# The end of a hybrid encoder layer's last projection: norm sums taken early, output scaling dealt out anew

## The chip, the cores and the metric

The kernel runs on one core of one Trainium2 chip. The metric is the device time of one launch in microseconds (us), lower is better. Five engines work side by side, each through its own list of instructions in order: TensorE (PE in the profile, with its weight loads as PEld), VectorE (DVE), ScalarE (ACT), GpSimd (POOL) and SyncE (SP), which here only issues transfers. They wait for each other by semaphores.

## The reference

One layer of a streaming encoder for two request groups, 256 + 128 = 384 tokens of width 2048, all in float32. What matters for this change is its last step, the MLP with a norm on its result:

```python
hdn = jnp.square(jax.nn.relu(rmsnorm(x, p['g_mlp_pre']) @ p['w_up'])) @ p['w_down']
x = x + rmsnorm(hdn, p['g_mlp_post'])

def rmsnorm(x, g):
    xf = x.astype(jnp.float32)
    y = xf * lax.rsqrt(jnp.mean(xf * xf, axis=-1, keepdims=True) + EPS)
    return (y * g.astype(jnp.float32)).astype(x.dtype)
```

`w_up` is 2048 x 8192 and `w_down` 8192 x 2048. The scale of a token needs the mean square over all its 2048 columns of `hdn`, so no column of the output can be finished before the last one is known.

## The kernel before

Every matrix product is made of three TensorE products of split operands (a high and a low part each), and the weights stream in from memory one after the other. The tokens lie in three blocks of 128, `b` = 0, 1, 2. The MLP runs in eight chunks of 1024 hidden columns. The first seven accumulate their part of `hdn` in device memory; the eighth, the "last down tile" of this document, is done at the end by `last_units` and brings everything together.

In `last_units` the output's 2048 columns are four column blocks `nb` = 0 to 3 of 512. For each there are four weight tiles `kp` of 256 hidden rows. For `nb` < 3 the three token blocks take turns on each weight tile. For `nb` = 3 only the first weight tile is used so; the other three are kept, and then token block 0 gets all its remaining products, then block 1, then block 2, so that the blocks finish one after the other. The products are lines 997 to 999 in the profile and the tiles are called `wd`.

`hacc[b][nb]` are twelve tiles of 128 x 512 that hold the sums of the first seven chunks (named `ac` in the profile); `tail` keeps what the end needs: `x1` (the layer's input to the MLP, `x1b` in the profile), `gpo` (the norm's gain), `st3` (one mean-square sum for each token block and column block) and a small pool, `lp2`.

`last_done(nb, bs, o)`, line 963, does for the given token blocks: on DVE the add of the product to the accumulated sum (line 966); on ACT the square with its sum over the columns into `st3` (969, two records, the second reads the accumulator); on DVE the multiplication by the gain, in place, after the square has read the tile (971). For `nb` = 3 it goes on for its one block: `postnorm` works out the scale, and then the four column tiles are scaled, added to `x1` and stored.

`postnorm`, line 671 on, makes the scale from `st3`: three one-element operations on DVE add up the first three sums (673 to 675, into `pre`), ACT takes the square root of the fourth sum with `pre` as bias (676), and DVE refines the reciprocal root by one Newton step (677 to 681). It is called for two earlier norms as well.

Scaling a tile is done in one of two ways. Either one DVE operation does `z * y + x1` (983), or ACT multiplies by the scale (980) and POOL adds `x1` (981). The line `if i >= (0, 2, 3)[b]` decides: block 0 has all four tiles on ACT and POOL, block 1 two and block 2 one; the others are on DVE. Each tile's store of 256 KB is issued by SP (984), in the order in which the code names them.

The order of instructions on every engine is that of the code: the whole MLP part runs under a manual schedule, so the code of a block stands on each engine ahead of the code of the next. TensorE has all products of the three blocks in its list, and nothing in the tail frees a buffer that it needs.

Of the kernel before, what the change touches and what calls it, by code (L numbers as in the profile page):

```python
# [6 lines left out]
F32 = mybir.dt.float32  # L7
F32R = mybir.dt.float32r
I32 = mybir.dt.int32
AF = mybir.ActivationFunctionType  # L10
ALU = mybir.AluOpType
# [3 lines left out]
P = 128  # L15
# [4 lines left out]
DM = 2048  # L20
# [3 lines left out]
EPS = 1e-6  # L24
# [10 lines left out]
def build(ctx, tc, io):  # L35
    nc = tc.nc
    v, s, te, gp, sy = nc.vector, nc.scalar, nc.tensor, nc.gpsimd, nc.sync
# [12 lines left out]
    def mmtile(name):  # L50
        return psm.tile([P, 512], F32, tag="mm", name=name)
# [9 lines left out]
    def wfetch(src, name):  # L61
        w = wpool.tile([P, 1024], F32, tag="w", name=f"w_{name}")
        sy.dma_start(w, src)
        return w, name
# [110 lines left out]
    l = wpool.tile([P, 1024], F32R, tag="wl", name="wl_p0_0")  # L175
# [28 lines left out]
    for k in range(KD):  # L204
        if k == 0:
            s.activation(acc, xr[0], AF.Square)
        else:
            q = pa.tile([P, T], F32, tag="sq", name=f"sq{k}")
# [8 lines left out]
    with tc.tile_pool(name="phc", bufs=1, reuse_waits="tile") as pc, tc.tile_pool(name="phc2", bufs=2, reuse_waits="tile") as pc2:  # L217
        pst = pc.tile([P, KD, NB, 15], F32, name="pst")
        gp.dma_start(pst, io["state_pool"])
        bufs = []  # L220
        for i in range(2):
            b = pc.tile([P, 519], F32, name=f"pbuf{i}")
# [148 lines left out]
    with tc.tile_pool(name="phd", bufs=2, reuse_waits="tile") as pd, tc.tile_pool(  # L371
        name="phd1", bufs=1, reuse_waits="tile"
    ) as pd1:
        bst = []
        for i in range(2):
            b = pd1.tile([P, 4, 2, P], F32R, name=f"bst{i}")
# [5 lines left out]
        for i in range(3):  # L382
            b = pd1.tile([P, 24, 19], F32, name=f"cbuf{i}")
# [34 lines left out]
        for g in range(G):  # L418
# [9 lines left out]
            for j in range(4):  # L428
                ps = proj(in_units(u0 + 6 + j), xg, f"z{g}_{j}")
                z = pd.tile([P, T], F32, tag="zs", name=f"zs{g}_{j}", bufs=7)  # L430
# [14 lines left out]
            bs = bst[g % 2]  # L445
# [22 lines left out]
            for j in range(4):  # L468
                nm = f"{g}_{j}"
# [59 lines left out]
                for sb, e0, c0, n in ((0, 0, 0, TP), (1, TP, P, P), (2, T, TP, P)):  # L529
# [13 lines left out]
                    out=x,  # L543
                    in0=x,
                    scalar=vec[:, V_DSK + g * 4 + j : V_DSK + g * 4 + j + 1],
                    in1=Y[:, :T],
                    op0=ALU.mult,
                    op1=ALU.add,
# [4 lines left out]
                else:  # L553
                    q = pd.tile([P, T], F32, tag="ysq", name=f"ysq{nm}", bufs=1)
# [58 lines left out]
    with tc.tile_pool(name="phe", bufs=1, reuse_waits="tile") as pe1, tc.tile_pool(name="phe2", bufs=3, reuse_waits="tile") as pe2:  # L613
        ab = []
        for i in range(32):
# [3 lines left out]
            l = pe1.tile([P, T], F32R, name=f"abl{i}")  # L619
# [3 lines left out]
        for n in range(KD):  # L623
# [8 lines left out]
            l = mp.tile([P, T], F32R, name=f"ml{n}")  # L632
# [10 lines left out]
    x1 = x1_pool.tile([P, 3, DM], F32, name="x1")  # L643
# [27 lines left out]
    def postnorm(pool, st, b, name):  # L671
        pre, ms, rt, y = (pool.tile([P, 1], F32, tag=f"n{i}", name=f"n{i}_{name}{b}", bufs=3) for i in range(4))
        v.tensor_tensor(pre, st[:, b, 0:1], st[:, b, 1:2], ALU.add)
        v.tensor_tensor(pre, pre, st[:, b, 2:3], ALU.add)
        v.tensor_scalar(pre, pre, 1.0 / DM, EPS, ALU.mult, ALU.add)
        root[0] = s.activation(rt, st[:, b, 3:4], AF.Sqrt, bias=pre, scale=1.0 / DM)
        v.tensor_scalar(ms, st[:, b, 3:4], 1.0 / DM, pre, ALU.mult, ALU.add)
        v.reciprocal(y, rt)
        v.tensor_scalar(ms, ms, y, y, ALU.mult, ALU.mult)
        v.tensor_scalar(ms, ms, -0.5, 1.5, ALU.mult, ALU.add)  # L680
        v.tensor_tensor(y, y, ms, ALU.mult)
        return y

    blk = lambda i: slice(i * 512, i * 512 + 512)
    for b in range(3):
        sy.dma_start(x1[:, b, :], io["x_tok"][b])
    with tc.tile_pool(name="phf", bufs=1, side="right", reuse_waits="tile") as pf, tc.tile_pool(
        name="phf2", bufs=2, side="right", reuse_waits="tile"
# [4 lines left out]
        for nb in range(4):  # L693
            gpo = pf2.tile([P, 512], F32, tag="gpo", name=f"gpo{nb}")
            sy.dma_start(gpo, io["g_mix_post"][blk(nb)].partition_broadcast(P))
            o = [mmtile(f"wo{nb}_{b}") for b in range(3)]
# [10 lines left out]
        for i in range(4):  # L707
            for b in range(3):
                xb = x1[:, b, blk(i)]
                if b == 1 and i >= 2:  # L710
# [5 lines left out]
                    out=xb, in0=hm[:, b, blk(i)], scalar=ys[b], in1=xb, op0=ALU.mult, op1=ALU.add  # L716
# [8 lines left out]
    for k in range(KD):  # L725
# [4 lines left out]
        l = pga.tile([P, T], F32R, name=f"x1l{k}")  # L730
# [5 lines left out]
    with tc.tile_pool(name="phn", bufs=1, side="right", reuse_waits="tile") as pn, tc.tile_pool(  # L736
        name="phn2", bufs=2, side="right", reuse_waits="tile"
    ) as pn2:
        st = pn.tile([P, 3, 4], F32, name="st2")
        for b in range(3):  # L740
            for i in range(4):
                q = pn2.tile([P, 512], F32, tag="q3", name=f"q2_{b}_{i}")
                s.activation(q, x1[:, b, blk(i)], AF.Square, accum_out=st[:, b, i : i + 1])
        dg = pn.tile([P, 3, P], F32, name="dg2")
        for b in range(3):
            y = postnorm(pn2, st, b, "n2")
# [17 lines left out]
    def split4(w, name):  # L764
        turn[0] += 1
        if turn[0] % DEPTH:
            return wsplit((w, name))
        h = pg.tile([P, 1024], F32R, tag="xh", name=f"wh_{name}")
        l = pg.tile([P, 1024], F32R, tag="xl", name=f"wl_{name}")
        s.activation(h, w, AF.Copy)  # L770
        v.tensor_tensor(l, w, h.bitcast(F32), ALU.subtract)
        return h, l
# [158 lines left out]
    ac, hacc, tail = [], [], {}  # L931
# [9 lines left out]
    def merge(p):  # L941
        a1, a2, a3, a4, a5, a6, a7 = ac[p][:7]
        v.tensor_tensor(a2, a1, a2, ALU.add)
        v.tensor_tensor(a6, a1, a6, ALU.add)
        v.tensor_tensor(a7, a6, a7, ALU.add)
        v.tensor_tensor(a4, a7, a4, ALU.add)
        v.scalar_tensor_tensor(out=a7, in0=a7, scalar=-1.0, in1=a5, op0=ALU.mult, op1=ALU.subtract)
        v.tensor_tensor(a6, a6, a5, ALU.add)
        v.scalar_tensor_tensor(out=a3, in0=a6, scalar=-1.0, in1=a3, op0=ALU.mult, op1=ALU.subtract)
# [10 lines left out]
        gp.dma_start(tail["gpo"], io["g_mlp_post"].partition_broadcast(P))  # L960
        gp.dma_start(tail["x1"], x1_scr)

    def last_done(nb, bs, o):
        lp2, st3, gpo = tail["lp2"], tail["st3"], tail["gpo"]
        for b in bs:
            v.tensor_tensor(hacc[b][nb], o[b], hacc[b][nb], ALU.add)
        for b in bs:
            q = lp2.tile([P, 512], F32, tag="q3", name=f"q3_{nb}_{b}")
            s.activation(q, hacc[b][nb], AF.Square, accum_out=st3[:, b, nb : nb + 1])
        for b in bs:  # L970
            v.tensor_tensor(hacc[b][nb], hacc[b][nb], gpo[:, blk(nb)], ALU.mult)
        if nb < 3:
            return
        for b in bs:
            y = postnorm(lp2, st3, b, "n3")
            for i in range(4):
                z = hacc[b][i]
                xb = tail["x1"][:, b, blk(i)]
                if i >= (0, 2, 3)[b]:
                    s.activation(z, z, AF.Copy, scale=y)  # L980
                    gp.tensor_tensor(z, z, xb, ALU.add)
                else:
                    v.scalar_tensor_tensor(out=z, in0=z, scalar=y, in1=xb, op0=ALU.mult, op1=ALU.add)
                sy.dma_start(io["y"][b][:, blk(i)], z)

    def last_units(hh):
        out = []
        for nb in range(4):
            o, kept = [], []

            def products(b, hl, kp, o=o):
                wh, wl = hl
                for k2 in range(2):
                    k = kp * 2 + k2
                    c = slice(k2 * 512, k2 * 512 + 512)
                    ah, al = hh[k][b]
                    te.matmul(o[b], ah, wh[:, c], start=k == 0, stop=False)
                    te.matmul(o[b], ah, wl[:, c], start=False, stop=False)
                    te.matmul(o[b], al, wh[:, c], start=False, stop=k == 7)

            for kp in range(4):

                def mm(hl, nb=nb, kp=kp, o=o, kept=kept, products=products):
                    if kp == 0:
                        o += [(sstile if nb % 2 else mmtile)(f"wd{c8}_{nb}_{b}") for b in range(3)]
                    if nb < 3 or kp == 0:
                        for b in range(3):
                            products(b, hl, kp)
                        return
                    kept.append(hl)  # L1010
                    if kp == 3:
                        for b in range(3):
                            for i, x in enumerate(kept):
                                products(b, x, i + 1)
                            last_done(nb, (b,), o)

                def post(nb=nb, kp=kp, o=o):
                    if nb < 2 and kp == 1:
                        merge(nb)
                    if nb < 3 and kp == 3:  # L1020
                        last_done(nb, range(3), o)

                out.append(
                    (
                        lambda nb=nb, kp=kp: wfetch(io["w_dlast"][nb, kp], f"wd{c8}_{nb}_{kp}"),
                        lambda w: split4(*w),
                        mm,
                        post,
                        False,
                    )  # L1030
                )
        return out
# [151 lines left out]
```

## Time and profile before

| | us |
|---|---|
| median of 3 runs | 2841.32 (2841.27 to 2841.41) |
| the profiled execution's own time | 2840.66 |
| its span, first to last recorded instruction | 2838.9 |
| DVE busy in the span | 1798.0 (63%) |
| ACT busy in the span | 1280.2 (45%) |
| POOL busy in the span | 254.8 (9%) |

How to read its rows. A timeline row gives the start of an instruction from the span's start, its length, engine, line of the code, operation, what it writes and reads, the tile's shape, how many follow each other, and in brackets the time that the engine sat idle before it and what ended that. In a merged row ("x3") the length runs from the first one's start to the last one's end. Following operations on one engine can overlap by a few hundredths of a microsecond. A row for one line of code gives the count, the shortest, median and longest length in ns, and the first and last start in us. For a transfer, the record is the issue alone; "DMA to landing" is the time from there until its data has arrived. The chain of waits names, for each piece of the time that set the end, who had it.

### The profile page before, as it was taken

The page shows a single profiled execution, that of the slowest core. Times are in us where ns is not written, and L with a number is a line of the kernel's source. Part 1 is how long each engine was busy: PE and PEld are TensorE (multiplying, and loading weights), DVE is VectorE, ACT ScalarE, POOL GpSimd, SP SyncE. Part 2 cuts the span into 40 slices and gives each one's busy share as a digit, 9 for nine tenths or more (in the row PEclk, how much of TensorE's full clock was granted, in tenths as well). Part 3 has the DMA queues.
Part 4 walks back from the last instruction along what each step waited for, and adds up shares of the span by engine and source line. Part 5 has one row for each costly group of instructions (what it writes and reads, how often), then busy time and mean ns, then how long its engine had stood idle before and what let it go on. Part 6 is the DMA issues. An engine that isn't in the chain of part 4 may idle for free.

```text
span 2838.9 us, 40540 instructions
## 1 busy us (share of the span) xinstructions
PE 2811.2 (99%) x15997; PEld 2655.9 (94%) x15997; DVE 1798.0 (63%) x2501; ACT 1280.2 (45%) x1869; POOL 254.8 (9%) x324
## 2 busy tenths in 40 slices
PE   9999999999999999999999999999999999999997
PEld 8999999999999999999999988899999999999996
DVE  7774335678678677677533333666767667676766
ACT  5443224445345445443522223545555455555543
POOL 0000000011011011011000000000111111111121
PEclk9999999999999999999999999999999999999999
DMA  6444445456465465465744453445666566666654
GB/s 215 132 135 138 138 141 194 146 202 215 151 212 200 155 221 189 161 232 189 240 149 154 149 182 130 151 164 189 184 167 163 160 164 158 180 183 186 175 157 195
DMA packets 160784, 492.90 MB, mean 174 GB/s; under 512 B 19809, under 2 KB 43553, under 8 KB 155729
## 3 DMA queue, kind: packets, MB, share of 16 engines
q1 hardware_dynamic: 133296, 410.14, 42.5%
q0 software_dynamic: 27296, 80.18, 11.6%
q8 instruction: 125, 2.05, 0.3%
q14 instruction: 67, 0.54, 0.1%
HBM read 412.34 MB, written 77.89 MB: 173 GB/s over the span
## 4 chain that ended last, share of the span: by engine, by line
PE 97%; DVE 1%; ACT 0%; issue 0%; DVEq 0%; ACTq 0%
PE pj_up L80 6%; PE pj_up L81 6%; PE pj_up L82 6%; PE pj_x L82 5%; PE pj_x L80 5%; PE pj_x L81 5%; PE wd L914 3%; PE pj_sp L80 3%; PE wd L916 3%; PE wd L915 3%; PE pj_z L82 3%; PE pj_z L80 3%; PE pj_sp L81 3%; PE pj_z L81 3%; PE pj_sp L82 3%; PE t L914 2%
## 5 line engine op out<-in xcount | busy, mean ns | idle before, releaser
L80 PE MATMUL pj_up<-x1h,wh_up 128*128 128x384 f32 x1024 | 345.6, 338 | 0.0
L81 PE MATMUL pj_up<-x1l,wh_up 128*128 128x384 f32 x1024 | 345.2, 337 | 0.0
L82 PE MATMUL pj_up<-x1h,wl_up 128*128 128x384 f32 x1024 | 344.7, 337 | 0.0
L80 PE MATMUL pj_x<-xgh,wh_x 128*128 128x384 f32 x768 | 261.4, 340 | 0.0
L82 PE MATMUL pj_x<-xgh,wl_x 128*128 128x384 f32 x768 | 258.3, 336 | 0.0
L81 PE MATMUL pj_x<-xgl,wh_x 128*128 128x384 f32 x768 | 256.8, 334 | 0.0
L73 DVE TENSOR_TENSOR wl_wd<-raw,wh_wd 128x1024 fp32r<-128x1024 f32 x168 | 202.3, 1222 | 68.8 <-ACT wh_wd L71 66.9
L71 ACT ACTIVATE wh_wd<-raw 128x1024 fp32r<-128x1024 f32 x168 | 175.1, 1054 | 96.9 <-PE pj_up L81 84.2
L80 PEld LDWEIGHTS pj_up<-x1h,wh_up 128*128 128x128 f32 x1024 | 192.8, 188 | 4.8 <-ACT x1h L732 0.4
L81 PEld LDWEIGHTS pj_up<-x1l,wh_up 128*128 128x128 f32 x1024 | 192.8, 188 | 4.5
L82 PEld LDWEIGHTS pj_up<-x1h,wl_up 128*128 128x128 f32 x1024 | 192.8, 188 | 0.1
L82 PE MATMUL pj_z<-xgh,wl_z 128*128 128x384 f32 x512 | 171.0, 334 | 0.0
L80 PE MATMUL pj_z<-xgh,wh_z 128*128 128x384 f32 x512 | 171.0, 334 | 0.0
L82 PE MATMUL pj_sp<-abh,wl_sp 128*128 128x384 f32 x512 | 171.0, 334 | 0.0
L81 PE MATMUL pj_z<-xgl,wh_z 128*128 128x384 f32 x512 | 171.0, 334 | 0.0
L80 PE MATMUL pj_sp<-abh,wh_sp 128*128 128x384 f32 x512 | 171.0, 334 | 0.0
L81 PE MATMUL pj_sp<-abl,wh_sp 128*128 128x384 f32 x512 | 171.0, 334 | 0.0
L73 DVE TENSOR_TENSOR wl_sp<-w_sp,wh_sp 128x1024 fp32r<-128x1024 f32 x64 | 78.3, 1224 | 118.9 <-ACT wh_sp L71 118.1
L882 POOL DMA_DIRECT2D acc_scr<-ev x108 | 92.7, 928 | 667.5 <-ACT ev L878 650.6
L80 PEld LDWEIGHTS pj_x<-xgh,wh_x 128*128 128x128 f32 x768 | 144.3, 188 | 2.5 <-issue 1.4
L82 PEld LDWEIGHTS pj_x<-xgh,wl_x 128*128 128x128 f32 x768 | 144.2, 188 | 2.6 <-issue 2.6
L81 PEld LDWEIGHTS pj_x<-xgl,wh_x 128*128 128x128 f32 x768 | 144.3, 188 | 1.1 <-issue 0.2
(335 smaller groups left out, 7112.4 us busy)
## 6 DMA issues: line engine op xcount, KB each, us to landing
w_up<-w_up SPq DMA_DIRECT2D x128, 512.0 KB, 4.4
raw<-w_down SPq DMA_DIRECT2D x112, 512.0 KB, 7.3
w_x<-w_in SPq DMA_DIRECT2D x96, 512.0 KB, 3.8
w_z<-w_in SPq DMA_DIRECT2D x64, 512.0 KB, 3.5
w_sp<-w_ssd SPq DMA_DIRECT2D x64, 512.0 KB, 3.5
acc_scr<-ev POOLq DMA_DIRECT2D x126, 256.0 KB, 4.6
w_ga<-w_in SPq DMA_DIRECT2D x32, 512.0 KB, 3.5
w_pp<-w_pp SPq DMA_DIRECT2D x32, 512.0 KB, 3.4
```

The lines of the kernel that those rows point to most:

```text
L71: s.activation(h, w, AF.Copy)
L73: v.tensor_tensor(l, w, h.bitcast(F32), ALU.subtract)
L80: te.matmul(out, wh, xh, start=first, stop=False)
L81: te.matmul(out, wh, xl, start=False, stop=False)
L82: return te.matmul(out, wl, xh, start=False, stop=last)
L882: gp.dma_start(acc_scr[p][r], e, accum_op=ALU.add)
L914: te.matmul(o, ah, wh[:, c], start=first, stop=False)
L915: te.matmul(o, ah, wl[:, c], start=False, stop=False)
L916: te.matmul(o, al, wh[:, c], start=False, stop=fin)
```

## The change

`last_done` is replaced by smaller functions, and the order in which they are called for the last column block is new.

- The three one-element operations that add up the first three mean-square sums of a block (`pre`) are taken out of the scale and done when the third column block (`nb` = 2) is done, each behind its block's gain: `last_early`, lines 978 to 980.
- For the last column block `last_scale` issues ACT's root first, then DVE's gain and the rest of the scale (985 to 991).
- The outputs are dealt out anew: column 0 of each block is scaled on DVE (1000) as soon as the scale is ready; columns 2 and 3 of blocks 0 and 1 go over ACT and POOL (997, 998); column 1 of blocks 0 and 1 goes over DVE, behind the next block's add (965); block 2 is done by DVE alone, in the order 0, 3, 1, 2. POOL has four adds in place of seven, ACT four scalings in place of seven, DVE eight scalings in place of five.
- The stores (1001) follow in the order in which the code names the tiles: column 1 of a block comes behind its other three.

The computation of each value is the same; sums and scalings are the same operations on the same operands.

```diff
-        if nb < 3:
-            return
-        for b in bs:
-            y = postnorm(lp2, st3, b, "n3")
-            for i in range(4):
-                z = hacc[b][i]
-                xb = tail["x1"][:, b, blk(i)]
-                if i >= (0, 2, 3)[b]:
-                    s.activation(z, z, AF.Copy, scale=y)
-                    gp.tensor_tensor(z, z, xb, ALU.add)
-                else:
-                    v.scalar_tensor_tensor(out=z, in0=z, scalar=y, in1=xb, op0=ALU.mult, op1=ALU.add)
-                sy.dma_start(io["y"][b][:, blk(i)], z)
+    def last_sums(nb, b, o):
+        lp2, st3 = tail["lp2"], tail["st3"]
+        v.tensor_tensor(hacc[b][nb], o[b], hacc[b][nb], ALU.add)
+        q = lp2.tile([P, 512], F32, tag="q3", name=f"q3_{nb}_{b}")
+        s.activation(q, hacc[b][nb], AF.Square, accum_out=st3[:, b, nb : nb + 1])
+
+    def last_gain(nb, b):
+        v.tensor_tensor(hacc[b][nb], hacc[b][nb], tail["gpo"][:, blk(nb)], ALU.mult)
...
+    def last_early(b):
+        st3 = tail["st3"]
+        pre = tail["pre", b] = small_("pre", b)
+        v.tensor_tensor(pre, st3[:, b, 0:1], st3[:, b, 1:2], ALU.add)
+        v.tensor_tensor(pre, pre, st3[:, b, 2:3], ALU.add)
+        v.tensor_scalar(pre, pre, 1.0 / DM, EPS, ALU.mult, ALU.add)
+
+    def last_scale(b):
+        st3, pre = tail["st3"], tail["pre", b]
+        rt, ms, y = (small_(nm, b) for nm in ("rt", "ms", "y"))
+        s.activation(rt, st3[:, b, 3:4], AF.Sqrt, bias=pre, scale=1.0 / DM)
+        last_gain(3, b)
+        v.tensor_scalar(ms, st3[:, b, 3:4], 1.0 / DM, pre, ALU.mult, ALU.add)
+        v.reciprocal(y, rt)
+        v.tensor_scalar(ms, ms, y, y, ALU.mult, ALU.mult)
+        v.tensor_scalar(ms, ms, -0.5, 1.5, ALU.mult, ALU.add)
+        v.tensor_tensor(y, y, ms, ALU.mult)
+        tail["y", b] = y
+
+    def last_out(b, i, split=False):
+        z, y, xb = hacc[b][i], tail["y", b], tail["x1"][:, b, blk(i)]
+        if split:
+            s.activation(z, z, AF.Copy, scale=y)
+            gp.tensor_tensor(z, z, xb, ALU.add)
+        else:
+            v.scalar_tensor_tensor(out=z, in0=z, scalar=y, in1=xb, op0=ALU.mult, op1=ALU.add)
+        sy.dma_start(io["y"][b][:, blk(i)], z)
+
+    def last_block(b, o):
+        last_sums(3, b, o)
+        if b:
+            last_out(b - 1, 1)
+        last_scale(b)
+        last_out(b, 0)
+        if b < 2:
+            last_out(b, 2, split=True)
+            last_out(b, 3, split=True)
+        else:
+            for i in (3, 1, 2):
+                last_out(b, i)
...
-                            last_done(nb, (b,), o)
+                            last_block(b, o)
...
                     if nb < 3 and kp == 3:
-                        last_done(nb, range(3), o)
+                        for b in range(3):
+                            last_sums(nb, b, o)
+                        for b in range(3):
+                            last_gain(nb, b)
+                            if nb == 2:
+                                last_early(b)
```

More of the change, by code (lines that the diff above doesn't have):

```diff
@@ L961, in enter_last @@
         gp.dma_start(tail["x1"], x1_scr)
-    def last_done(nb, bs, o):
-        lp2, st3, gpo = tail["lp2"], tail["st3"], tail["gpo"]
-        for b in bs:
[L966 to L971, printed above, removed]
-        if nb < 3:
-            return
-        for b in bs:
-            y = postnorm(lp2, st3, b, "n3")
-            for i in range(4):
-                z = hacc[b][i]
-                xb = tail["x1"][:, b, blk(i)]
-                if i >= (0, 2, 3)[b]:
-                    s.activation(z, z, AF.Copy, scale=y)
-                    gp.tensor_tensor(z, z, xb, ALU.add)
-                else:
-                    v.scalar_tensor_tensor(out=z, in0=z, scalar=y, in1=xb, op0=ALU.mult, op1=ALU.add)
-                sy.dma_start(io["y"][b][:, blk(i)], z)
+    def last_sums(nb, b, o):
[3 more added lines that the diff above has]
+        s.activation(q, hacc[b][nb], AF.Square, accum_out=st3[:, b, nb : nb + 1])
@@ new lines, in last_gain, with small_ @@
+    def last_gain(nb, b):
+        v.tensor_tensor(hacc[b][nb], hacc[b][nb], tail["gpo"][:, blk(nb)], ALU.mult)
+    def small_(nm, b):
+        return tail["lp2"].tile([P, 1], F32, tag=f"l{nm}", name=f"l{nm}{b}", bufs=3)
+    def last_early(b):
[4 more added lines that the diff above has]
+        v.tensor_scalar(pre, pre, 1.0 / DM, EPS, ALU.mult, ALU.add)
```

## The prediction

> **What bounds the kernel now.** I read the page's first and fourth parts, then, engine by engine, the timeline from 2806 us on, the rows of single lines of code, and the landing of the stores.
>
> ```profile
> span 2838.9 us, 40540 instructions
> ...
> PE 97%; DVE 1%; ACT 0%; issue 0%; DVEq 0%; ACTq 0%
> ```
>
> ```profile
> 2816.68 0.39 PE L999 MATMUL wd<-wh_wd,hl 128*128 128x512 f32 x1
> ...
> 2820.76 0.39 PE L999 MATMUL wd<-wh_wd,hl 128*128 128x512 f32 x1
> ```
>
> TensorE carries 97% of the chain, but its last products for token blocks 1 and 2 (the second fence, start and length) end at 2817.07 and 2821.15. The span runs on to 2838.9, so 17.75 us at the end belong to other engines, and only there can this change act: the order of TensorE's instructions and of their waits is the same in both programs, and no other engine's differs ahead of this tail. Its rows, DVE first, then ACT:
>
> ```profile
> 2808.90 1.89 DVE L971 TENSOR_TENSOR ac<-ac,gpo 128x512 f32<-128x512 f32 x3
> 2813.03 0.69 DVE L966 TENSOR_TENSOR ac<-wd,ac 128x512 f32<-128x512 f32 x1 [2.24 <-PE wd L999]
> 2814.57 0.69 DVE L971 TENSOR_TENSOR ac<-ac,gpo 128x512 f32<-128x512 f32 x1 [0.85 <-ACT q L969]
> 2815.18 0.15 DVE L673 TENSOR_TENSOR n_n<-st 128x1 f32<-128x1 f32 x1
> ...
> 2815.75 0.22 DVE L677 TENSOR_SCALAR n_n<-st,n_n 128x1 f32<-128x1 f32 x1
> 2816.14 0.16 DVE L678 RECIPROCAL n_n<-n_n 128x1 f32<-128x1 f32 x1 [0.17 <-ACT n_n L676]
> ...
> 2817.11 0.69 DVE L966 TENSOR_TENSOR ac<-wd,ac 128x512 f32<-128x512 f32 x1
> 2820.24 0.69 DVE L971 TENSOR_TENSOR ac<-ac,gpo 128x512 f32<-128x512 f32 x1 [2.44 <-ACT q L969]
> 2820.86 1.22 DVE L673 TENSOR_TENSOR n_n<-st 128x1 f32<-128x1 f32 x1
> 2822.11 1.18 DVE L674 TENSOR_TENSOR n_n<-n_n,st 128x1 f32<-128x1 f32 x1
> ...
> 2824.79 1.41 DVE L983 SCALAR_TENSOR_TENSOR ac<-ac,n_n,x1b 128x512 f32<-128x512 f32 x2
> 2826.12 0.68 DVE L966 TENSOR_TENSOR ac<-wd,ac 128x512 f32<-128x512 f32 x1
> 2827.60 1.50 DVE L971 TENSOR_TENSOR ac<-ac,gpo 128x512 f32<-128x512 f32 x1 [0.79 <-ACT q L969]
> ...
> 2830.86 3.08 DVE L983 SCALAR_TENSOR_TENSOR ac<-ac,n_n,x1b 128x512 f32<-128x512 f32 x3
> ```
>
> ```profile
> 2813.82 0.63 ACT L969 ACTIVATE q<-ac 128x512 f32<-128x512 f32 x1 [3.98 <-DVE ac L966]
> 2814.36 0.18 ACT L969 ACTIVATION_READ_ACCUMULATOR q<-ac 128x1 f32 x1
> 2815.81 0.29 ACT L676 ACTIVATE n_n<-st,n_n 128x1 f32<-128x1 f32 x1 [1.27 <-DVE n_n L675]
> 2817.03 2.56 ACT L980 ACTIVATE ac<-ac,n_n 128x512 f32<-128x512 f32 x4 [0.92 <-DVE n_n L681]
> 2819.50 0.62 ACT L969 ACTIVATE q<-ac 128x512 f32<-128x512 f32 x1
> ```
>
> Call y0, y1, y2 the moments when a block's scale is ready: 2817.03, 2824.79 and 2830.86, where its first scaling starts. Block 1 is late twice. Its square (2819.50) stands behind block 0's four scalings on ACT, though its input was ready at 2817.80; and two of its one-element sums took 1.22 and 1.18 us where block 0's took 0.15. The POOL rows say why.
>
> ```profile
> 2817.84 1.29 POOL L981 TENSOR_TENSOR ac<-ac,x1b 128x512 f32<-128x512 f32 x1 [44.77 <-ACT ac L980]
> ...
> 2820.35 2.93 POOL L981 TENSOR_TENSOR ac<-ac,x1b 128x512 f32<-128x512 f32 x2
> 2822.02 1.25 POOL L981 TENSOR_TENSOR ac<-ac,x1b 128x512 f32<-128x512 f32 x1
> 2825.59 1.74 POOL L981 TENSOR_TENSOR ac<-ac,x1b 128x512 f32<-128x512 f32 x1 [2.31 <-ACT ac L980]
> 2827.30 1.26 POOL L981 TENSOR_TENSOR ac<-ac,x1b 128x512 f32<-128x512 f32 x1
> 2831.66 1.74 POOL L981 TENSOR_TENSOR ac<-ac,x1b 128x512 f32<-128x512 f32 x1 [3.11 <-ACT ac L980]
> ```
>
> POOL's add and a DVE operation with two operands in SBUF never progress together. The sums of 2820.86 and 2822.11 end at 2822.08 and 2823.29, where POOL's adds end (2822.02, 2823.27). The gain of 2827.60 ends at 2829.10, 0.54 after the add that ends at 2828.56; the last scaling ends at 2833.94, 0.54 after POOL's 2833.40. The other way round, POOL's add of 2820.35 ends at 2822.02, 1.09 after the gain that ends at 2820.93. They take turns: whoever waits goes next, even if the other has more queued (add, sum, add, sum from 2820.35 to 2823.29). L966 of 2826.12, with one operand in PSUM, ran its usual 0.68 beside POOL: it isn't held.
>
> ```profile
> L984 SPq DMA_DIRECT2D y<-ac x2: 332/358/383, 2834.0 to 2834.4; - x2
> ...
> DMA to landing us min/median/max: 2.1/2.3/2.4
> ```
>
> The end: the last scaling is done at 2833.94, its store goes out at once, that of POOL's block right behind at 2834.4 and lands 2.4 later, at 2836.8; closing takes 2.1 more, to 2838.9.
>
> **The change part by part.** (1) The nine one-element sums (L978 to L980) move ahead of block 0's last product, between the gains of the third column block. DVE was idle for 2.24 us there. Three take 2815.18 to 2815.75, 0.57, so 1.71 in all; gains and sums then end near 2812.5, and DVE waits until 2813.03 as before. Cost nothing, with 0.5 us to spare; without that cover 1.7. POOL had been idle for 44.77 us until 2817.84, so the price of a held sum doesn't apply.
>
> (2) Block 0: add 2813.03, square 2813.82, accumulator read until 2814.54. The root (L985) no longer waits for DVE's sums; at 0.29 it is over before 2815.0. On DVE the gain stays at 2814.57 and L987 follows at 2815.18. From there to the reciprocal I take 0.25 (L677's 0.22 and a small gap), 2815.43; from the reciprocal to the first use of the scale it was 2817.03 less 2816.14, 0.89. So y0 is 2816.32, 0.71 earlier: the sums' 0.57 and 0.14 of waiting for the root.
>
> (3) Block 0's outputs. DVE writes column 0 at once, 2816.32 to 2817.06; a scaling lasts 0.74 and the next begins 0.67 later (the pair's 1.41). ACT scales columns 2 and 3 only, until 2817.65. POOL's first add starts 0.81 after y0, as 2817.84 after 2817.03: 2817.13 to 2818.40. Block 1's add still waits for TensorE, 2817.11. Now the new order: column 1's scaling (L1000) stands between that add and block 1's gain on DVE, with block 1's whole scale queued behind it. Ready at 2817.73, it is held by POOL until 2818.40 and ends 0.55 later, 2818.95. POOL's second add, waiting since 2818.40, goes next and ends 1.10 later, 2820.05. The gain of block 1, which its square (now 2817.90) frees at 2818.65, is held by that add and ends at 2820.60. Its follower starts 0.07 ahead of that end, 2820.53 (as 2815.18 lies ahead of 2815.26); reciprocal 0.25 on, y1 0.89 on: 2821.67. From y0 that is 5.35, against 7.76 before.
>
> (4) Block 1 does the same: column 0 at 2821.67, block 2's add at 2822.34 (its product is ready at 2821.15), POOL's third add 2822.48 to 2823.75, column 1 held and done at 2824.30, fourth add to 2825.40, gain of block 2 done at 2825.95, y2 at 2827.02. Again 5.35, against 6.07.
>
> (5) Block 2: ACT and POOL do nothing, DVE scales four columns with nobody beside it, from 2827.02, 2827.69, 2828.36 and 2829.03, and ends at 2829.77. Before, three scalings and POOL's add took until the store at 2834.4, 3.54 after y2; now the last store goes out at 2829.80, 2.78 after y2.
>
> (6) Stores: still twelve of 256 KB in one queue, in the new order of results, column 1 of a block behind both POOL columns; its store goes out about 1 us late, on which nothing depends.
>
> The last pair of before landed in 2.1 and 2.4, the second standing 0.4 behind the first. The new last four leave 0.67 apart, so I take 2.2 for the last, bounds 2.1 and 2.6 (0.2 more for a queue four deep).
>
> Sum: 0.71 + 2.41 + 0.72 + 0.76 = 4.60 until the last store, and 0.2 in its landing: 4.8 us. Against the profiled execution's own 2840.66 (span 2838.9) that makes 2835.9; the three runs shown have their median, 2841.32, 0.66 above it, so 2836.5.
>
> The held sum of 1.22 us beside a free one of 0.15 is the row on which this rests. The Trainium skill, "SBUF — State Buffer", Who interferes with whom, has the rule: a DVE instruction with two SBUF inputs and a GpSimd instruction that reads SBUF shut each other out, and the second to issue blocks until the first is done. It speaks against a scaling on DVE laid between POOL's adds, and the trace agrees with it. By it the sum is the 4.8 above; were the two engines free of each other, the same steps without the holds (1.27 in each of two blocks) would give 7.3 and 2834.0.
>
> **The rivals.** First: DVE keeps its turn, so that the gain follows the scaling at once and POOL's second add comes after it. Then the gain runs 2818.88 to 2819.57, POOL's add to 2820.67, and y1 is 2820.76, held only by L991 waiting for POOL's end; y2 likewise 2825.19; the last scaling ends at 2827.94, 1.83 earlier, and the time is 2834.7. For it: the gain is ready before the scaling ends. Against: the turns above, and the last scaling of before, which lost its turn to POOL although it stood directly behind its forerunner.
>
> Second: POOL does both adds in one go before DVE gets in. Column 1 then ends at 2820.20, y1 is 0.21 later and y2 0.41: 2836.9. Against it: the sum of 2820.86 came in between two adds.
>
> Third, slower: POOL's adds run long. It has a row:
>
> ```profile
> L556 POOL TENSOR_TENSOR ssum<-ssum,ysq x24: 1002/2964/3033, 552.5 to 1327.6; 128x384 f32<-128x384 f32 x24
> ```
>
> A smaller add took 3.03 there. In the new order all four adds lie on the chain to y2; at 3.03 instead of 1.25 each costs 1.78, 7.1 in all, less 4.8 gained: 2.3 slower, 2843.6. It decides from 2.45 us an add on. Against: the adds of this very shape took 1.25 free and 1.74 at most, DVE's share included.
>
> Fourth: the change doesn't do what it says, since the early sums push block 0's add. Then at most 1.7 is lost again, 2838.2; the 2.24 idle speaks against it.
>
> **How the numbers follow.** Forecast 0.73, first rival 0.14, second 0.07, third 0.04, fourth 0.02. The likeliest is 2836.5. The range, 2834.6 to 2838.0, holds the first two rivals, the landing's bounds and the 0.66 by which executions of one kernel differ here; it leaves out the third, the fourth's end and small remainders of the others. 0.2%, 5.7 us, is about what a measurement of this kernel can tell from no change: the limits are 2835.6 and 2847.0. Faster, 0.2: the first rival's 0.14 and 0.06 of the forecast, where its terms are 0.9 too small. Slower, 0.02: the third at over 3.9 us an add. The rest, 0.78, lies within.
>
> **What would show it.** DVE's add of block 0 still at 2813.0 (else step 1 is wrong); the root ended before the gain, y0 0.7 earlier; one scaling of 1.2 us in each of blocks 0 and 1 and a gain of about 1.7 behind it (step 3; gains of 0.69 mean the first rival); y0 to y1 and y1 to y2 both 5.35; four scalings 0.67 apart at the end and no POOL work after 2825.4; last store at 2829.8, landed in 2.2. Adds over 2.4 us, or a stall outside this tail, would make it wrong.

## The result, and the profile after

The changed kernel takes 2835.57 us (median of 16 runs, 2834.52 to 2837.07) against 2841.15 for the one before (16 runs, 2840.32 to 2841.89): the ratio is 0.9981, with a 95% interval of 0.9973 to 0.9988. That is 5.6 us or 0.19%, just inside the 0.2% that was taken as the limit of "no change", and with an interval that excludes 1. Forecast were 2836.5 and a range of 2834.6 to 2838.0.

The profiled execution of the changed kernel has a span of 2834.2. Its tail on DVE, from the first block's last product on, by the timeline (start and length in us; x4 is four instructions in a row, from the start of the first to the end of the last):

```profile
2812.85 0.15 DVE L980 TENSOR_SCALAR lpre<-lpre 128x1 f32<-128x1 f32 x1
2813.90 0.69 DVE L965 TENSOR_TENSOR ac<-wd,ac 128x512 f32<-128x512 f32 x1 [0.90 <-PE wd L1029]
2815.44 0.69 DVE L970 TENSOR_TENSOR ac<-ac,gpo 128x512 f32<-128x512 f32 x1 [0.85 <-ACT q L967]
2816.05 0.20 DVE L987 TENSOR_SCALAR lms<-st,lpre 128x1 f32<-128x1 f32 x1
2816.18 0.15 DVE L988 RECIPROCAL ly<-lrt 128x1 f32<-128x1 f32 x1
...
2817.06 0.75 DVE L1000 SCALAR_TENSOR_TENSOR ac<-ac,ly,x1b 128x512 f32<-128x512 f32 x1
2817.98 0.69 DVE L965 TENSOR_TENSOR ac<-wd,ac 128x512 f32<-128x512 f32 x1 [0.17 <-PE wd L1029]
2818.59 1.12 DVE L1000 SCALAR_TENSOR_TENSOR ac<-ac,ly,x1b 128x512 f32<-128x512 f32 x1
2819.63 1.77 DVE L970 TENSOR_TENSOR ac<-ac,gpo 128x512 f32<-128x512 f32 x1
...
2822.14 0.16 DVE L991 TENSOR_TENSOR ly<-ly,lms 128x1 f32<-128x1 f32 x1
2822.33 0.75 DVE L1000 SCALAR_TENSOR_TENSOR ac<-ac,ly,x1b 128x512 f32<-128x512 f32 x1
2823.00 0.68 DVE L965 TENSOR_TENSOR ac<-wd,ac 128x512 f32<-128x512 f32 x1
2823.60 1.34 DVE L1000 SCALAR_TENSOR_TENSOR ac<-ac,ly,x1b 128x512 f32<-128x512 f32 x1
2824.87 1.75 DVE L970 TENSOR_TENSOR ac<-ac,gpo 128x512 f32<-128x512 f32 x1
...
2827.34 0.16 DVE L991 TENSOR_TENSOR ly<-ly,lms 128x1 f32<-128x1 f32 x1
2827.54 2.74 DVE L1000 SCALAR_TENSOR_TENSOR ac<-ac,ly,x1b 128x512 f32<-128x512 f32 x4
```

The early sums end at 2813.00 and DVE still waits 0.90 for the product: they are free. The three scales are ready at 2817.06, 2822.33 and 2827.54. Two instructions in each of blocks 0 and 1 are longer than the 0.7 that they need: the scaling of column 1 (1.12, 1.34), and the gain behind it (1.77, 1.75). What they wait for is seen on POOL:

```profile
2817.86 1.29 POOL L998 TENSOR_TENSOR ac<-ac,x1b 128x512 f32<-128x512 f32 x1 [41.34 <-ACT ac L997]
2819.13 1.73 POOL L998 TENSOR_TENSOR ac<-ac,x1b 128x512 f32<-128x512 f32 x1
2823.13 2.94 POOL L998 TENSOR_TENSOR ac<-ac,x1b 128x512 f32<-128x512 f32 x2 [2.27 <-ACT ac L997]
```

POOL's first add ends at 2819.15; the scaling of 2818.59 ends 0.56 later, 2819.71. POOL's second add, on record from 2819.13, ends at 2820.86, 1.15 after that scaling; the gain of 2819.63 ends at 2821.40, 0.54 after that. Scaling and adds take turns, as read from the profile of before.

The stores, by the row of line 1001 and by the last one alone (the second fence, of the rows after 2830):

```profile
L1001 SPq DMA_DIRECT2D y<-ac x12: 332/332/432, 2817.8 to 2830.3; - x12
```

```profile
L1001 SPq DMA_DIRECT2D y<-ac x1: 332/332/332, 2830.3 to 2830.3; - x1
...
DMA to landing us min/median/max: 2.2/2.2/2.2
```

The last store goes out at 2830.3 and lands at 2832.5; 1.7 us later the span ends.

The body ahead of the tail isn't equally long in two executions: DVE's add of block 0 started at 2813.03 before and at 2813.90 here, and between 2812.60 and 2814.35 in the runs below, with the same products up to there. So the tail is measured from that add. To the last store it took 21.4 us before (2834.4 less 2813.03) and 16.4 now; to the end of the span 25.87 and 20.30. The difference of the second pair, 5.57, is that of the medians, 5.58. An agreement to 0.01 is partly luck, but in all eight kernels of the next section that have a median, the median less the tail lies between 2814.7 and 2815.4: what differs between them is the tail.

### The profile page after: what moved, and what is told of

It is laid out like the page before. It is cut to its first block, busy times and chain, and to the rows that moved or that the text cites. A ratio compares the mean times of both kernels' runs of the same rounds, so it can differ in the third digit from the quotient of the medians.

```text
span 2834.2 us, 40535 instructions
## 1 busy us (share of the span) xinstructions
PE 2811.6 (99%) x15997; PEld 2655.8 (94%) x15997; DVE 1797.7 (63%) x2504; ACT 1278.2 (45%) x1866; POOL 251.2 (9%) x321
## 4 chain that ended last, share of the span: by engine, by line
PE 97%; DVE 1%; DMA 0%; ACT 0%; issue 0%; SPq 0%; DVEq 0%; ACTq 0%
PE pj_up L80 6%; PE pj_up L81 6%; PE pj_up L82 6%; PE pj_x L82 5%; PE pj_x L80 5%; PE pj_x L81 5%; PE wd L914 3%; PE pj_sp L80 3%; PE wd L916 3%; PE pj_z L82 3%; PE wd L915 3%; PE pj_z L80 3%; PE pj_sp L81 3%; PE pj_z L81 3%; PE pj_sp L82 3%; PE t L914 2%
```

## The experiments

Two theories. **Turns**: an operation of DVE with two operands in SBUF and an add of POOL exclude each other and alternate, and the gain is what the new order saves in such holds and in the sums. **Work taken off**: the gain comes from seven scalings and adds on ACT and POOL becoming four, and what stands beside POOL is merely somewhat slower. All figures of the table are from one profile each, from the add of block 0; the medians stand beside the kernel before of the same session (2841.04 for the first four runs, 2841.57 for the other four).

| kernel | last store, us | end of span, us | median, us | ratio to before, 95% interval |
|---|---|---|---|---|
| before | 21.4 | 25.87 | 2841.15 | |
| sums early only | 18.2 | 22.70 | 2837.39 | 0.9988 (0.9979 to 0.9997) |
| new dealing only | 18.9 | 22.86 | 2838.23 | 0.9990 (0.9981 to 0.9999) |
| changed kernel | 16.4 | 20.30 | 2835.57 | 0.9981 (0.9973 to 0.9988) |
| block 2's column 3 split again | 17.2 | 21.65 | 2836.85 | 0.9984 (0.9975 to 0.9993) |
| column 1 behind the scale | 16.4 | 20.35 | one run, 2835.15 | |
| all scalings on DVE | 16.1 | 19.94 | 2834.85 | 0.9978 (0.9969 to 0.9987) |
| the same, gain from PSUM | 16.0 | 19.86 | one run, 2835.59 | |
| gain from PSUM | 14.2 | 18.27 | 2833.07 | 0.9973 (0.9962 to 0.9983) |
| gain and column 3 from PSUM | 14.0 | 17.91 | 2832.82 | 0.9970 (0.9959 to 0.9981) |

### Each part of the change alone

Sums early, the outputs dealt out as before:

```diff
     def last_block(b, o):
         last_sums(3, b, o)
-        if b:
-            last_out(b - 1, 1)
         last_scale(b)
...
+        for i in range(4):
+            last_out(b, i, split=i >= (0, 2, 3)[b])
```

> The kernel before with one part of the change: the sums of the first three mean squares early, the dealing of the outputs as before. Measured from DVE's add of block 0 to the issue of the last store (21.4 us before, 16.4 in the changed kernel). Turns theory (a DVE operation with two SBUF operands and an add of POOL exclude each other): each held sum of 1.2 us in block 1 goes, the gain of block 1 is held once by POOL's fourth add instead; last store at 18.2, 3.2 us faster than before. Rival (the change gains by taking work off ACT and POOL, and an operation beside POOL is only a little slower): three sums of 0.19 and 0.14 of waiting for the root in each block, 0.7 for the one block whose sums are on the path, at most 2.1 for all three; last store at 19.3 to 20.7.

Measured: last store at 18.2 (2830.8 less 2812.60), as the turns theory said and earlier than the rival's 19.3. From the timeline, DVE in block 1, then POOL:

```profile
2818.97 0.70 DVE L970 TENSOR_TENSOR ac<-ac,gpo 128x512 f32<-128x512 f32 x1 [1.60 <-ACT q L967]
...
2820.21 0.16 DVE L990 TENSOR_SCALAR lms<-lms 128x1 f32<-128x1 f32 x1
2820.40 0.44 DVE L991 TENSOR_TENSOR ly<-ly,lms 128x1 f32<-128x1 f32 x1
2820.88 3.39 DVE L1000 SCALAR_TENSOR_TENSOR ac<-ac,ly,x1b 128x512 f32<-128x512 f32 x2
```

```profile
2816.57 8.82 POOL L998 TENSOR_TENSOR ac<-ac,x1b 128x512 f32<-128x512 f32 x6 [40.98 <-ACT ac L997]
```

The two sums of 1.2 are gone from here; what is left of POOL's adds now holds the last step of the scale (0.44 instead of 0.16) and then the two scalings, 3.39 for a pair that took 1.41 before. POOL adds without a pause from 2816.57 to 2825.39, yet the step just ahead of the held one (L990), with a single tensor operand, keeps its 0.16: here the number of tensor operands decides, not the size. The expectation had the gain held; it wasn't, it came late because its square still stands behind four scalings on ACT (1.60 of waiting). So the sum was right and the instruction named for it only in part.

The new dealing with the sums put back behind each gain:

```diff
     def last_scale(b):
+        last_gain(3, b)
+        last_early(b)
         st3, pre = tail["st3"], tail["pre", b]
...
-        last_gain(3, b)
...
                             last_gain(nb, b)
-                            if nb == 2:
-                                last_early(b)
```

> The changed kernel with the sums put back behind each block's gain, so that only the new dealing of the outputs is left. Turns theory: 0.8 us later in each of the three scales, last store at 19.0 after block 0's add, 2.4 us faster than before, and with the early sums' 3.2 the two parts together come to somewhat more than the 5.0 of both. Rival (work taken off ACT and POOL is what gains): nearly everything is kept, last store at about 17.1, 4.3 faster than before.

```profile
2817.45 0.75 DVE L1001 SCALAR_TENSOR_TENSOR ac<-ac,ly,x1b 128x512 f32<-128x512 f32 x1
...
2823.57 0.75 DVE L1001 SCALAR_TENSOR_TENSOR ac<-ac,ly,x1b 128x512 f32<-128x512 f32 x1
...
2829.61 2.74 DVE L1001 SCALAR_TENSOR_TENSOR ac<-ac,ly,x1b 128x512 f32<-128x512 f32 x4
```

Measured: 18.9 to the last store. From scale to scale it takes 6.12 and 6.04 instead of 5.27 and 5.21: the sums cost 0.8 in each scale even where nothing holds them, and the dealing alone is worth 2.4, not 4.3. The two parts, 3.2 and 2.4, make 5.6, against 5.0 together: each of them alone already rids block 1 of its held sums.

### What ACT and POOL are still worth

All twelve scalings on DVE:

```diff
         if b < 2:
-            last_out(b, 2, split=True)
-            last_out(b, 3, split=True)
+            last_out(b, 2)
+            last_out(b, 3)
```

> The changed kernel with all twelve scalings on DVE; ACT's four scalings and POOL's four adds of the tail are gone. Turns theory: POOL's adds took DVE's time one for one where they met, so nothing is lost: no held instruction is left, y1 and y2 come 0.1 earlier or later, last store at 16.4 after block 0's add, the same as the changed kernel to 0.3 us. Rival (ACT and POOL carry real work beside DVE): four scalings more on DVE at 0.67 each, last store at 19.1, 2.7 slower.

```profile
2816.82 2.08 DVE L1000 SCALAR_TENSOR_TENSOR ac<-ac,ly,x1b 128x512 f32<-128x512 f32 x3
2818.81 0.68 DVE L965 TENSOR_TENSOR ac<-wd,ac 128x512 f32<-128x512 f32 x1
2819.41 0.74 DVE L1000 SCALAR_TENSOR_TENSOR ac<-ac,ly,x1b 128x512 f32<-128x512 f32 x1
2820.29 0.69 DVE L970 TENSOR_TENSOR ac<-ac,gpo 128x512 f32<-128x512 f32 x1
...
2821.90 2.08 DVE L1000 SCALAR_TENSOR_TENSOR ac<-ac,ly,x1b 128x512 f32<-128x512 f32 x3
```

DVE does two scalings more in each of blocks 0 and 1, and the next scale comes after 5.08 us (2816.82 to 2821.90) instead of 5.27. Nothing is held: 0.74 and 0.69 in place of 1.12 and 1.77. The last store goes out 0.3 earlier and the span ends 0.4 earlier, which is about what the expectation allowed, where the rival had the last store 2.7 later. So in the changed kernel the four scalings on ACT and four adds on POOL gain nothing; by the profiles they take from DVE a little more than they give, which the intervals of the two kernels don't tell apart.

Block 2's column 3 on ACT and POOL again:

```diff
-            for i in (3, 1, 2):
-                last_out(b, i)
+            for i in (1, 2, 3):
+                last_out(b, i, split=i == 3)
```

> The changed kernel with block 2's column 3 back on ACT and POOL, as before the change; the rest of the new dealing stays. Turns theory: y2 is unmoved, the third scaling of block 2 is held by POOL's add (1.7 instead of 0.75), the last two stores go out 0.4 apart; last store 17.1 us after block 0's add (16.4 in the changed kernel), and 0.2 more until it has landed, 0.7 to 1.3 us slower in all. Rival (ACT and POOL beside DVE shorten the last block): one scaling of 0.67 less on DVE, last store at 15.8 to 16.0.

```profile
2827.98 3.08 DVE L1000 SCALAR_TENSOR_TENSOR ac<-ac,ly,x1b 128x512 f32<-128x512 f32 x3
```

```profile
2828.78 1.74 POOL L998 TENSOR_TENSOR ac<-ac,x1b 128x512 f32<-128x512 f32 x1 [2.27 <-ACT ac L997]
```

DVE (first fence) takes 3.08 for three scalings, longer than the 2.74 for four without POOL: its third scaling was held by POOL's add (second fence), as the turns theory said. The last store is 0.8 later and the span's end 1.35: landing and closing take 4.5 us together instead of 3.9. What lengthens them is shown at the end of the section on the prediction.

### The order, and the hold itself

Column 1's scaling behind the next block's scale instead of ahead of its gain:

```diff
-        if b:
-            last_out(b - 1, 1)
         last_scale(b)
+        if b:
+            last_out(b - 1, 1)
```

> The changed kernel with column 1's scaling of blocks 0 and 1 put behind the next block's scale instead of ahead of its gain. Turns theory: block 1's gain is held by POOL's second add only for what is left of it, y0 to y1 is 0.4 shorter (4.9 instead of 5.27), but the scaling itself moves onto the path behind each scale, five scalings stand at the end; last store at 16.7, 0.3 slower than the changed kernel. Rival (the scaling ahead of the gain is what holds blocks 1 and 2 back): y1 and y2 0.4 and 0.8 earlier, last store at 15.6.

Neither number came: the last store stayed at 16.4, against 16.7 and 15.6.

```profile
2816.21 0.75 DVE L1000 SCALAR_TENSOR_TENSOR ac<-ac,ly,x1b 128x512 f32<-128x512 f32 x1
...
2818.61 1.49 DVE L970 TENSOR_TENSOR ac<-ac,gpo 128x512 f32<-128x512 f32 x1 [0.79 <-ACT q L967]
...
2820.83 0.16 DVE L991 TENSOR_TENSOR ly<-ly,lms 128x1 f32<-128x1 f32 x1
2820.91 1.41 DVE L1000 SCALAR_TENSOR_TENSOR ac<-ac,ly,x1b 128x512 f32<-128x512 f32 x2
...
2823.71 1.50 DVE L970 TENSOR_TENSOR ac<-ac,gpo 128x512 f32<-128x512 f32 x1 [0.79 <-ACT q L967]
...
2825.93 0.16 DVE L991 TENSOR_TENSOR ly<-ly,lms 128x1 f32<-128x1 f32 x1
2826.01 3.39 DVE L1000 SCALAR_TENSOR_TENSOR ac<-ac,ly,x1b 128x512 f32<-128x512 f32 x5
```

The first scaling behind each scale here is column 1's, which needs only the scale of the block before; so the scales are timed by their last step, L991. The gain is held for 0.8 instead of 1.1 and the scaling not at all, so that L991 comes 4.62 and 9.72 after block 0's first scaling, against 5.08 and 10.28 in the changed kernel: 0.46 and then 0.56 earlier in all. The turns theory had expected 0.4 of this. The fifth scaling at the end, 0.65, takes it back. In one profile of each, the order between scaling and gain is a draw.

Now the hold of the gain is taken away, with as little else as possible. For the last column block the sum is written back to the product's own tile in PSUM, and square and gain read it there, so the gain has one operand in SBUF:

```diff
     def last_block(b, o):
-        last_sums(3, b, o)
+        last_o[0] = o
+        v.tensor_tensor(o[b], o[b], hacc[b][3], ALU.add)
+        q = tail["lp2"].tile([P, 512], F32, tag="q3", name=f"q3_3_{b}")
+        s.activation(q, o[b], AF.Square, accum_out=tail["st3"][:, b, 3:4])
...
-        last_gain(3, b)
+        v.tensor_tensor(hacc[b][3], last_o[0][b], tail["gpo"][:, blk(3)], ALU.mult)
```

> The changed kernel, in which the last column block's sum is kept in PSUM: the add writes back to the product's tile, the square and the gain read it there, so the gain has one SBUF operand. Turns theory: the gains of blocks 1 and 2 (1.77 and 1.75 us in the changed kernel) take 0.7 beside POOL's second add, y0 to y1 and y1 to y2 shrink from 5.25 to 4.2, last store at 14.4 after block 0's add, 2.0 us faster than the changed kernel. Rival (an operation beside POOL is slow whatever it reads, or the gain waits for its square): gains still 1.7, last store at 16.4, no change.

DVE, then POOL, by the timeline:

```profile
2816.95 0.75 DVE L1002 SCALAR_TENSOR_TENSOR ac<-ac,ly,x1b 128x512 f32<-128x512 f32 x1
...
2818.52 1.08 DVE L1002 SCALAR_TENSOR_TENSOR ac<-ac,ly,x1b 128x512 f32<-128x512 f32 x1
2819.52 0.68 DVE L988 TENSOR_TENSOR ac<-wd,gpo 128x512 f32<-128x512 f32 x1
...
2821.12 0.75 DVE L1002 SCALAR_TENSOR_TENSOR ac<-ac,ly,x1b 128x512 f32<-128x512 f32 x1
2821.99 0.70 DVE L1007 TENSOR_TENSOR wd<-wd,ac 128x512 f32<-128x512 f32 x1
...
2823.66 0.68 DVE L988 TENSOR_TENSOR ac<-wd,gpo 128x512 f32<-128x512 f32 x1
```

```profile
2817.76 2.99 POOL L1000 TENSOR_TENSOR ac<-ac,x1b 128x512 f32<-128x512 f32 x2 [41.60 <-ACT ac L999]
```

The gain of 2819.52 takes 0.68 in the middle of POOL's two adds (until 2820.75), where the changed kernel's took 1.77; POOL does no less than there. The scaling ahead of it, still with two SBUF operands, is still held (1.08). From scale to scale it takes 4.17 (2816.95 to 2821.12) instead of 5.27, the last store at 14.2, 2.2 earlier.

The control, with all scalings on DVE, where POOL does nothing in the tail (the edit is the one of "all scalings on DVE", made on this kernel):

> All scalings on DVE and the gain read from PSUM: a control for the gain from PSUM where POOL does nothing. Turns theory: nothing was held, so nothing is won; last store at 16.0 after block 0's add, as with all scalings on DVE and the gain from SBUF. Rival (reading and writing PSUM is itself quicker, or the shorter wait for the square is what gained): 2 us faster, last store at 14.0.

Last store at 16.0, against 16.1 with the gain from SBUF: PSUM by itself is worth 0.1 at most. The 2.2 us were POOL's holds.

Last, column 3 is kept in PSUM for its scaling as well and takes column 1's place ahead of the next gain:

```diff
-        v.tensor_tensor(hacc[b][3], last_o[0][b], tail["gpo"][:, blk(3)], ALU.mult)
+        v.tensor_tensor(last_o[0][b], last_o[0][b], tail["gpo"][:, blk(3)], ALU.mult)
...
-            v.scalar_tensor_tensor(out=z, in0=z, scalar=y, in1=xb, op0=ALU.mult, op1=ALU.add)
+            v.scalar_tensor_tensor(out=z, in0=last_o[0][b] if i == 3 else z, scalar=y, in1=xb, op0=ALU.mult, op1=ALU.add)
...
-            last_out(b - 1, 1)
+            last_out(b - 1, 3)
...
+            last_out(b, 1, split=True)
             last_out(b, 2, split=True)
-            last_out(b, 3, split=True)
```

> The kernel with the gain read from PSUM, and column 3 kept there for its scaling too; column 3 takes the place of column 1 ahead of the next block's gain, POOL gets columns 1 and 2. Turns theory: that scaling has one SBUF operand, so it takes 0.75 beside POOL's first add instead of 1.1; block 2's add already waits for its product, so only some 0.1 in y1 and 0.1 to 0.2 in y2 are left to win: last store at 13.9 after block 0's add (14.2 with the gain alone). Rival (operations beside POOL slow down whatever they read): still 1.1, last store at 14.2.

```profile
2818.68 0.74 DVE L1002 SCALAR_TENSOR_TENSOR ac<-wd,ly,x1b 128x512 f32<-128x512 f32 x1
2819.52 0.70 DVE L988 TENSOR_TENSOR wd<-wd,gpo 128x512 f32<-128x512 f32 x1
...
2822.15 0.70 DVE L1007 TENSOR_TENSOR wd<-wd,ac 128x512 f32<-128x512 f32 x1 [0.26 <-PE wd L1034]
```

The scaling beside POOL's first add now takes 0.74, and block 2's add waits for TensorE again (0.26). The last store is at 14.0 (13.9 expected). Here POOL's adds do help: 14.0 against 16.0 with DVE alone. This kernel, 2832.82, is the fastest of all, 8.7 us below the kernel before of its session; 0.4 us of tail over the gain from PSUM alone is seen in the profiles, but not told apart by the runs.

## Why the prediction was right

**Step 1, the early sums**: right. They cost nothing; DVE had 0.90 left, where 0.5 was reckoned. The early sums alone bring 3.2 of the 5.0 to the last store.

**Step 2, block 0's scale**: right in kind, small in size. y0 came 3.16 after the add instead of 4.00: 0.84 earlier, not 0.71. The reciprocal starts 0.13 after L987, where the prediction took 0.25.

**Steps 3 and 4, the holds**: right. Forecast were a scaling of 1.2, a gain of 1.7 behind it and 5.35 from scale to scale; measured 1.12 and 1.34, 1.77 and 1.75, and 5.27 and 5.21. The two scales again contain that 0.12. Who goes next was the point on which the first two rivals turned: the second add of POOL went between scaling and gain in both blocks, as forecast. The kernel with the gain from PSUM shows that the wait was for POOL, and what it cost.

**Step 5, block 2 on DVE alone**: right. Four scalings took 2.74, the last store 2.76 after y2 (2.78 forecast); splitting one off again cost 0.8 at the last store.

**Step 6 and the sum**: the step that was mis-sized. Against the forecast 4.60 the last store came 4.97 earlier (21.37 less 16.40), three times the 0.12 of the reciprocal. Behind the last store the prediction had 0.2 for the landing and nothing for the closing. The landing was 2.2 instead of 2.4 as forecast, but the closing took 1.7 instead of 2.1. Together 5.57 instead of 4.8, which is the whole distance between 2836.5 and the measured 2835.57, but for 0.2 between the medians of before.

The rule of the Trainium skill ("SBUF — State Buffer", Who interferes with whom), that a DVE instruction with two SBUF inputs contends with a GpSimd instruction that reads SBUF and one with at most one, outside certain modes, doesn't, agrees with the pairs of records shown here: holds of up to 1.1 us where both operands are in SBUF, none (0.68 and 0.74) where one is in PSUM. The slower rivals found nothing: POOL's adds took 1.27 and 1.29 free and 1.73 with DVE's share.

The closing, which the prediction put behind the last landing as a fixed 2.1, has a cause that the traces show. On the line that closes the program POOL has a DRAIN, whose record begins before its last add is over; before, in the changed kernel, and with block 2's column 3 split again:

```profile
L1166 POOLq DRAIN x1: 6472/6472/6472, 2831.6 to 2831.6; - x1
```

```profile
L1201 POOLq DRAIN x1: 7062/7062/7062, 2823.7 to 2823.7; - x1
```

```profile
L1201 POOLq DRAIN x1: 6475/6475/6475, 2828.7 to 2828.7; - x1
```

In all eight kernels in which POOL adds in the tail this record ends 4.70 us after POOL's last add. Before, the last add ended at 2833.40, the DRAIN at 2838.10, which is 1.3 after the last landing, and the span 0.79 later. The same 0.79 is seen in all three kernels in which POOL works on block 2 (before, sums early only, column 3 split again), and only there was the closing 2.1. In the other seven POOL's DRAIN is over 2.5 us or more ahead of the span's end, and the closing is 1.6 to 1.7. So in the kernel before it was POOL's last add, and not the last store, from which the end followed, and 0.4 of the 5.57 us comes from taking POOL off block 2. Why the DRAIN ends so long after the add isn't shown.

## What to carry to other kernels

Before giving POOL a share of DVE's elementwise work, count DVE's instructions with two SBUF operands that fall beside it: here each waited for what was left of an add, up to 1.1 us, and even a one-element sum did. Work dealt out to POOL paid here only where DVE had something to do meanwhile that reads PSUM: four adds were worth nothing with the gain's operands in SBUF, and 2 us with one of them in PSUM. POOL's last add belongs well ahead of the end as well, since the end of the program followed it by 5.5 us (4.70 and 0.79). Small operations that need only early data belong ahead of the last wait, and in a tail of 20 us it pays to write the list of each engine with its holds by hand: the sum came within 0.4 us at the last store.

## What the runs showed that was not expected

- Landing and closing behind the last store take 3.9 to 4.1 us in seven kernels and 4.5 in the three in which POOL works to the end: there POOL's DRAIN, 4.70 us behind its last add, is over last.
- An add that writes its result back to PSUM takes 0.70 us, as long as one that writes to SBUF (0.69), and the square that reads it there is followed by the gain no later: 1.51 from add to gain, against 1.54.
- The time until the tail's first add differs by up to 1.75 us between profiled executions of kernels that are the same up to there; a change of a few us in the tail is read from the tail's own clock first.
